# Down projections with more Strassen pairs, whose weight sums are made during the up projections and kept in HBM

## The chip, the cores and the metric

The kernel runs on one core of one Trainium2 chip. The metric is the device time of one execution in microseconds (us). The core has a matrix engine (TensorE, PE in the profile; PEld is its weight load), a vector engine (VectorE, DVE), a scalar engine (ScalarE, ACT), GpSimd (POOL, unused here) and SyncE (SP), whose queue issues the transfers between HBM and the on-chip memory (SBUF). Matmul results accumulate in PSUM.

## The reference

A two-layer encoder on 256 tokens of width 2048 in float32. Each layer is a token mixer followed by a channel mixer, both between RMS norms. Only the channel mixer is touched:

```python
def conv_glu(h, w_up, conv_w, conv_b, w_down):
    u = h @ w_up                                   # 2048 -> 2 * 5632
    gate, val = u[..., :D_FF], u[..., D_FF:]
    gate = depthwise_conv3(gate, conv_w, conv_b)
    return (jax.nn.gelu(gate, approximate=False) * val) @ w_down   # 5632 -> 2048

for i in range(DEPTH):
    ...
    x = x + rms_norm(m, p['mix_post'])
    h = rms_norm(x, p['ffn_pre'])
    x = x + rms_norm(conv_glu(h, *p['ffn']), p['ffn_post'])
```

## The kernel before

Every product is made to nearly full float32 precision from reduced-precision matmuls (type fp32r): each operand is split into a high part and the rest, `hi` and `lo`, and three products are added: hi·hi, hi·lo and lo·hi. The activations are split once. The weights are split as they come in, and this feeds TensorE through the whole program:

- All weights are cut into chunks of 128 rows by 1024 columns (512 KB); `all_chunks` lists them in the order of their use. A chunk holds two blocks of 128x512.
- `_load` lets SyncE fetch a chunk into one of four `raw` buffers (line 162). `_split` casts it on ScalarE into one of five `whi` buffers (line 187) and lets VectorE subtract that from `raw` into one of five `wlo` buffers (line 182). After the subtraction the `raw` buffer is free for the next load; after the chunk's last matmul the `whi` and `wlo` buffers are.
- `weights` is called once a chunk. It issues the splits of up to three chunks and the loads of three more, and hands out the current one. SyncE takes its waits and loads in the order of issue; the order in which an engine gets its other work is set when the program is built.
- `tick`, called after each chunk, runs one step of every generator that was registered with `now`. In this way the vector work of one stage is laid beside the matmuls of another.

The feed-forward block `ffn` runs 11 column groups of 512 (`NFG`). For each, `proj_t` makes the gate half and the value half, with eight chunks each and 16 matmuls a chunk (lines 263 and 265); then VectorE and ScalarE make convolution, GELU and product, and split the result into `gh` and `gl`, the operands of the down projection.

`down` multiplies by the 5632x2048 weights. The 44 row blocks form 22 pairs; the 2048 columns form two halves (`h`) of two column groups (`o`); the tokens form two tiles of 128 (`t`). For one pair and one half this is a 2x2 by 2x2 block product. Plain, it takes eight block products, that is 24 matmuls (lines 1264, 1265 and 1267), from two chunks. By Strassen's rule in Winograd's form it takes seven, 21 matmuls, and needs four sums of weight blocks and four sums of token blocks:

- The class `Seven` loads the two chunks of a pair into buffers of their own (`seven_a`, `seven_b` or `yf`, line 67). Step 0 uses a chunk as it is; then VectorE makes the four weight sums in place (line 81), and steps 1 to 3 use them. So there are 3.5 chunks to split, from two loads.
- `sums` makes the token sums on VectorE, for two pairs at a time, into the tiles `seven`.
- `down_order` writes the order of the chunks out by hand: `LEAD` plain chunks, then for each pair its steps 0 to 3 with plain chunks (`None`) between, then the plain chunks that are left. `PAIRS` says how many of the 22 pairs go by Strassen's rule, by layer and half. The last five chunks of a layer (`HELD`) run one token tile after the other.
- `added` combines the four PSUM banks that Strassen's rule adds, and `done` finishes a half; both are VectorE and ScalarE work that is registered at the last Strassen chunk of the half.

Of the kernel before, what the change touches and what calls it, by code (L numbers as in the profile page):

```python
# [17 lines left out]
P = 128  # L18
# [18 lines left out]

PAIRS = (6, 6), (6, 7)
LEAD = 5, 1


def down_order(h, pairs):

    plain = [("plain", p, o) for o in range(2) for p in range(pairs, KF // 2)]
    out, plain = plain[:LEAD[h]], deque(plain[LEAD[h]:])
    for p in range(pairs):
        for j in (0, None, 1, None, 2, None, 3) if h else (0, None, None, 1, None, 2, 3, None):
            out.append(plain.popleft() if j is None else ("seven", p, j))
    return out + list(plain)


class Seven:

    def __init__(self, a, b):
        self.srcs, self.raw = (a, b), None

    def load(self, model):
        if self.raw is None:
            self.raw = []
            for src, tag in zip(self.srcs, "ab"):
                home = "yf" if tag == "b" and next(model.turns) % 2 else f"seven_{tag}"
                raw = model.room.tile([P, 1024], F32, tag=home, name=f"seven_{tag}", bufs=1)
                model.nc.sync.dma_start(out=raw, in_=src)
                self.raw.append(raw)

    def step(self, model, j):  # L70

        a, b = self.raw
        return (a, a, b, self.t2)[j] if j else a

    def sums(self, model):
        nc = model.nc
        a, b = self.raw
        self.t2 = model.room.tile([P, 512], F32, tag="seven_t", name="seven_t", bufs=1)
        a0, a1, b0, b1 = a[:, :512], a[:, 512:], b[:, :512], b[:, 512:]
        for out, x, y in ((a0, b0, a0), (self.t2, b1, a0), (a1, a1, self.t2), (b0, b1, b0)):  # L80
            nc.vector.tensor_tensor(out=out, in0=x, in1=y, op=ALU.subtract)  # L81


# [8 lines left out]
class Model:  # L92
# [6 lines left out]
    def __init__(self, ctx, tc, a, out):  # L99
        self.tc, self.nc, self.a, self.out = tc, tc.nc, a, out  # L100
        self.soon, self.bg, self.running = [], deque(), []
        self.held = deque()
        self.gate, self.lead, self.led = (), None, 8
        pool = lambda name, **k: ctx.enter_context(tc.tile_pool(name=name, **k))
        self.const = pool("const", bufs=1)
        self.act = pool("act", bufs=1)
        self.wp = pool("wp", bufs=1)
        self.small = pool("small", bufs=2)
        self.ps = pool("ps", bufs=4, space=bass.MemoryType.PSUM)


# [42 lines left out]
    def _load(self, i):  # L154
        if i >= len(self.chunks) or i in self.loaded or i < self.at or i in self.made:
            return
        if isinstance(self.chunks[i], tuple):
            self.chunks[i][0].load(self)
            self.loaded[i] = None
            return  # L160
        raw = self.wp.tile([P, 1024], F32, tag="raw", name="raw", bufs=4)
        self.nc.sync.dma_start(out=raw, in_=self.chunks[i])
        self.loaded[i] = raw

    def _split(self, i, parts=1, late=False):
# [3 lines left out]
        raw = self.loaded.pop(i)  # L169
        seven, step = self.chunks[i] if raw is None else (None, 0)  # L170
        if seven:
            raw = seven.step(self, step)
        if i in self.spot:
# [5 lines left out]

        def low(s=slice(0, 1024)):  # L180
            nc = self.nc
            return nc.vector.tensor_tensor(out=lo[:, s], in0=raw[:, s], in1=hi[:, s].bitcast(F32), op=ALU.subtract)  # L182

        with self.behind(self.gate):
            for j in range(parts):
                s = slice(n * j, n * j + n)
                self.nc.scalar.copy(hi[:, s], raw[:, s])  # L187
                if not late:
                    low(s)
        if seven and step == 0:  # L190
            seven.sums(self)
        self.made[i] = (hi, lo)
# [203 lines left out]
    def spread(self, sp):  # L396

        nc = self.nc
        pb = self.psum("acc")
        for t in range(2):  # L400
            nc.tensor.matmul(pb[:, t * P:(t + 1) * P], self.r[:, t:t + 1].broadcast_to([P, P]), self.ident,
                             start=True, stop=True)
        self.rb = sp.tile([P, T], F32, tag="rb", name="rb", bufs=1)
        nc.vector.tensor_copy(self.rb, pb[:, :T])
# [708 lines left out]
    def ffn(self, layer, pre):  # L1113
        nc, tc = self.nc, self.tc
        with tc.tile_pool(name=f"ffn{layer}", bufs=1) as sp:
            self.room = sp
            xs = self.xhl
            x = lambda k: xs[k // 4][:, k % 4].rearrange("p a t -> p (a t)")
            gh = [sp.tile([P, 4, T], F32R, tag=f"gh{i}", name=f"gh{i}") for i in range(NFG)]
            gl = [sp.tile([P, 4, T], F32R, name=f"gl{i}") for i in range(NFG)]  # L1120
            cw = lambda j, c: self.gain(f"l{layer}_conv_w", j * KF + c)
            gw = sp.tile([P, 4, T], F32, tag="gw", name="gw", bufs=1)
            self.turns = count()
            norm = self.now(self.pre_norm(sp))
            for gi in range(NFG):
                pg = self.proj_t(KD, x, "acc", ROWS[layer] if gi == 0 else 0, gi == 0)
                self.finish(norm)
# [18 lines left out]
                if gi:  # L1146
                    gates()
                pv = self.proj_t(KD, x, "at", after=None if gi else gates)
                for i in range(4):
                    u = self.joined(gw[:, 2 + i % 2], sp.tile([P, T], F32, tag="u", name="u", bufs=2), pv[i])  # L1150
# [3 lines left out]
            self.down(gh, gl, 2 * layer + 1, pre)  # L1154

    def down(self, gh, gl, post, pre):
# [7 lines left out]

        def sums():

            most = max(many)
            for i in range((most + 1) // 2):
                q = min(2, most - 2 * i)
                if q == 1:  # L1170
                    for _ in range(16):
                        yield
                tmp = self.act.tile([P, 2, 512 * q], F32, tag="xm3", name="sums")
                add(tmp[:, 0], gh[i][:, :2 * q].rearrange("p k t -> p (k t)").bitcast(F32),
                    gl[i][:, :2 * q].rearrange("p k t -> p (k t)").bitcast(F32))
                a = tmp[:, 0].rearrange("p (q k t f) -> p q k t f", q=q, k=2, t=2)
# [6 lines left out]
                yield  # L1183
                home, tag = (self.act, f"xm{i}") if i < 3 else (self.room, "gw")
                seven.append(home.tile([P, q, 4, 2, P], F32R, tag=tag, name=f"seven{i}"))
                self.parted(seven[i][:, :, :, 0, :], seven[i][:, :, :, 1, :], s)
                yield
# [4 lines left out]
        def summed(p, n):  # L1192
            return tuple(seven[p // 2][:, p % 2, n, i, :] for i in range(2))

        def operands(kind, p, j, t):

            if kind == "plain":
                return [(2 * j + t, lambda k=2 * p + i: tokens(k, t), i) for i in range(2)]
            if t:
                return []  # L1200
            return [[(4, lambda: tokens(2 * p, 0), 0), (0, lambda: tokens(2 * p + 1, 0), 1)],
                    [(5, lambda: summed(p, 0), 0), (1, lambda: tokens(2 * p + 1, 1), 1)],
                    [(7, lambda: summed(p, 2), 0), (2, lambda: summed(p, 3), 1)],
                    [(6, lambda: summed(p, 1), 0)]][j]

# [31 lines left out]
        gains.append(self.gain_row(post, 0))  # L1237
        self.now(sums())
        ended = None
        for h in range(2):  # L1240
# [29 lines left out]
            for i in range(n):  # L1270
                if i == units[0]:
                    banks += [self.psum("at") for _ in range(4)]
                w = self.weights()
                while items[i][0] == "seven" and len(seven) <= items[i][1] // 2:
                    self.tick()
# [8 lines left out]
            if h == 0:  # L1284
# [49 lines left out]
    def all_chunks(self):  # L1334
# [4 lines left out]

        def down(w, many):  # L1340
            items = []
            for h in range(2):
                pairs = [Seven(w[2 * h, p], w[2 * h + 1, p]) for p in range(many[h])]
                items += [w[2 * h + j, p] if kind == "plain" else (pairs[p], j)
                          for kind, p, j in down_order(h, many[h])]
            return items

        ffn = lambda l: groups(a[f"w_up{l}"], [g for j in range(NFG) for g in (j, NFG + j)]) + \
            down(a[f"w_down{l}"], PAIRS[l])
        out += ffn(0)  # L1350
# [11 lines left out]
def _tiled(w, n=512):  # L1362
# [3 lines left out]
    w = w.reshape(k // (b * P), b, P, m // n, n).transpose(3, 0, 2, 1, 4)  # L1366
    return np.ascontiguousarray(w).reshape(m // n, k // (b * P), P, 1024)


# [57 lines left out]
```

## Time and profile before

| | |
|---|---|
| median of 3 runs | 2049.87 us (2049.73 to 2050.01) |
| the profiled execution | 2049.89 us; span of its instructions 2048.1 us |
| mean granted TensorE clock | 0.998 |
| up projections of layer 0 and 1 | about 344 to 820 us and 1333 to 1810 us |
| down projections of layer 0 and 1 | about 820 to 1058 us and 1810 to 2040 us |
| HBM read, written | 381.96 MB, 2.10 MB |

Times in the profile are in microseconds unless marked ns. "L182" is line 182 of the kernel. In a list of groups a row gives line, engine, operation, the tile written and those read, shapes and count, then the total busy time and the mean duration in ns, and after the bar the engine's idle time just before these instructions and what ended it. In a list of waits a row gives who waited for whom, then us in total, number and longest. A timeline row gives start and length in us, and "x2" means two merged instructions.

### The profile page before, as it was taken

How to read it: one execution, taken by the hardware profiler on the slowest of the kernel's cores; microseconds unless marked ns; L12 is line 12 of the kernel's file. 1: busy time of each engine (PE TensorE's matmuls, PEld its weight loads, DVE VectorE, ACT ScalarE, POOL GpSimd, SP SyncE). 2: the span in 40 equal slices, each digit the busy share in tenths (PEclk: the TensorE clock that was granted, in tenths of full speed). 3: DMA queues.
4: the chain of work that ended last, by engine and by line, in shares of the span. 5: the costliest groups of instructions: out<-in, count | busy, mean ns of one | idle time of the engine just before them, and what ended most of it. 6: DMA issues, size and time to landing. Idle time of an engine off the chain costs nothing.

```text
span 2048.1 us, 29263 instructions
## 1 busy us (share of the span) xinstructions
PE 2035.5 (99%) x10927; PEld 1749.3 (85%) x10927; DVE 1487.1 (73%) x2296; ACT 1133.9 (55%) x1780; POOL 0.2 (0%) x4
## 2 busy tenths in 40 slices
PE   9999999999999999999999999999999999999998
PEld 7888888888888888888888998888888888888886
DVE  6877757766766767978777875676766766797886
ACT  7654546555555555555555664565555555555553
POOL 0000000000000000000000000000000000000000
PEclk9999999999999999999999999999999999999999
DMA  9555566666666666566556445566666666656663
GB/s 335 180 150 161 165 198 201 189 194 193 185 194 189 185 194 191 189 207 211 190 162 188 136 130 171 176 223 190 185 194 193 186 193 190 193 176 216 197 215 122
DMA packets 108718, 385.97 MB, mean 188 GB/s; under 512 B 12064, under 2 KB 12576, under 8 KB 108576
## 3 DMA queue, kind: packets, MB, share of 16 engines
q1 hardware_dynamic: 108288, 383.83, 60.1%
q8 instruction: 85, 1.39, 0.3%
q14 instruction: 57, 0.47, 0.1%
q10 hardware_dynamic: 288, 0.28, 0.0%
HBM read 381.96 MB, written 2.10 MB: 188 GB/s over the span
## 4 chain that ended last, share of the span: by engine, by line
PE 99%; DVE 0%; ACT 0%; DMA 0%; issue 0%; DVEq 0%; SPq 0%
PE ps L263 31%; PE ps L265 15%; PE ps L248 8%; PE ps L246 8%; PE ps L247 8%; PE ps L1265 8%; PE ps L1267 8%; PE ps L1264 8%; PE ps L674 1%; PE ps L332 1%; PE ps L577 1%; PE ps L504 0%; PE ps L584 0%; DMA raw<-in_w_in 0%; PE ps L1004 0%; ACT xhl L727 0%
## 5 line engine op out<-in xcount | busy, mean ns | idle before, releaser
L182 DVE TENSOR_TENSOR wlo<-raw,whi 128x1024 fp32r<-128x1024 f32 (+1 forms) x650 | 792.1, 1221 | 449.8 <-ACT whi L187 444.8
L187 ACT CAST whi<-raw 128x1024 fp32r<-128x1024 f32 (+1 forms) x650 | 681.4, 1050 | 595.8 <-PE ps L263 323.8
L263 PE MATMUL ps<-xhl,whi 128*128 128x512 f32 x2752 | 952.6, 394 | 0.0
L265 PE MATMUL ps<-xhl,wlo 128*128 128x256 f32 x2752 | 757.5, 277 | 0.0
L263 PEld LDWEIGHTS ps<-xhl,whi 128*128 128x128 f32 x2752 | 513.9, 188 | 116.9
L265 PEld LDWEIGHTS ps<-xhl,wlo 128*128 128x128 f32 x2752 | 516.7, 188 | 2.6
L1264 PE MATMUL ps<-whi,gh 128*128 128x512 f32 x579 | 225.5, 389 | 0.0
L1265 PE MATMUL ps<-whi,gl 128*128 128x512 f32 x579 | 225.3, 389 | 0.0
L1267 PE MATMUL ps<-wlo,gh 128*128 128x512 f32 x579 | 180.2, 389 | 0.0
L246 PE MATMUL ps<-whi,xhl 128*128 128x512 f32 x336 | 132.3, 395 | 1.6 <-ACT whi L187 1.6
L247 PE MATMUL ps<-wlo,xhl 128*128 128x512 f32 x336 | 131.4, 391 | 0.0
L248 PE MATMUL ps<-whi,xhl 128*128 128x512 f32 x336 | 130.9, 391 | 0.1
L1264 PEld LDWEIGHTS ps<-whi,gh 128*128 128x128 f32 x579 | 108.7, 188 | 22.6
L1267 PEld LDWEIGHTS ps<-wlo,gh 128*128 128x128 f32 x579 | 108.7, 188 | 22.6
L1265 PEld LDWEIGHTS ps<-whi,gl 128*128 128x128 f32 x579 | 108.7, 188 | 22.4
L246 PE MATMUL ps<-whi,oh 128*128 128x512 f32 x256 | 100.3, 392 | 0.0
L247 PE MATMUL ps<-wlo,oh 128*128 128x512 f32 x256 | 99.7, 390 | 0.0
L248 PE MATMUL ps<-whi,ol 128*128 128x512 f32 x256 | 99.7, 389 | 0.0
L336 ACT COPY gw<-ps 128x256 f32<-128x256 f32 x176 | 64.8, 370 | 42.8 <-PE ps L263 33.8
L187 ACT CAST whi<-seven_a 128x1024 fp32r<-128x1024 f32 x50 | 52.7, 1053 | 62.6 <-DVE seven_a L81 35.3
L182 DVE TENSOR_TENSOR wlo<-seven_a,whi 128x1024 fp32r<-128x1024 f32 x50 | 61.1, 1223 | 20.7 <-ACT whi L187 19.1
L246 PEld LDWEIGHTS ps<-whi,xhl 128*128 128x128 f32 x336 | 63.1, 188 | 14.2 <-ACT whi L187 1.8
(230 smaller groups left out, 2195.4 us busy)
## 6 DMA issues: line engine op xcount, KB each, us to landing
raw<-in_w_up SPq DMA_DIRECT2D x352, 512.0 KB, 4.2
raw<-in_w_down SPq DMA_DIRECT2D x126, 512.0 KB, 4.3
raw<-in_w_in SPq DMA_DIRECT2D x88, 512.0 KB, 4.4
raw<-in_w_out SPq DMA_DIRECT2D x64, 512.0 KB, 3.7
seven_a<-in_w_down SPq DMA_DIRECT2D x25, 512.0 KB, 4.8
seven_b<-in_w_down SPq DMA_DIRECT2D x25, 512.0 KB, 5.2
gb<-in_post SPq DMA_DIRECT2D x16, 256.0 KB, 3.9
raw<-in_w_qn SPq DMA_DIRECT2D x8, 512.0 KB, 3.6
```

Of the source, the lines that this page charges most:

```text
L182: return nc.vector.tensor_tensor(out=lo[:, s], in0=raw[:, s], in1=hi[:, s].bitcast(F32), op=ALU.subtract)
L187: self.nc.scalar.copy(hi[:, s], raw[:, s])
L246: mm(ps, lh, rh, start=start, stop=False)
L247: mm(ps, lh, rl, start=False, stop=False)
L248: return mm(ps, ll, rh, start=False, stop=stop)
L263: ins = mm(out[i], hi[:, s[kk]], x(k), start=k == 0, stop=False, skip_group_check=opening)
L265: ins = mm(out[i][:, :T], lo[:, s[kk]], x(k)[:, :T], start=False, stop=k == nk - 1, skip_group_check=opening)
L332: self.tc.keep_in_program_order(self.nc.tensor.transpose(out, x, self.ident))
L336: self.nc.scalar.copy(b, ps[:, T:])
L1264: mm(bank, xh, w[0][:, c], start=start, stop=False, skip_group_check=loose)
L1265: mm(bank, xl, w[0][:, c], start=False, stop=False, skip_group_check=loose)
L1267: ins = mm(bank, xh, w[1][:, c], start=False, stop=stop, skip_group_check=loose)
```

## The change

The weight sums are made earlier. In `ffn`, from the second column group on, the generator `block_sums` runs beside the up projections, one step a chunk. For every Strassen pair of the layer's down projection it loads the pair's two chunks (1 MB) into one of two buffers (`st` and `g_last`), makes the four sums in place in three VectorE subtractions, and stores both halves in HBM (`blocks`); a job takes seven steps, and two jobs overlap. Host-side, `_paired` lays the four blocks of a pair in one row. In `down` a Strassen pair then has four chunks like any other, all loaded into `raw`: step 0 the two blocks as they are, steps 1 and 2 the stored sums, step 3 one block alone (half a chunk). The class `Seven` goes.

`PAIRS` goes from (6, 6), (6, 7) to (9, 11), (9, 11). In the second half, from the fourth pair on, one plain chunk stands among a pair's steps; elsewhere two do. The token sums for nine pairs are made at the start of `down`, those of two more at the turn of the halves, in `raw` buffers. To find room, `rb` and `u` share the tile `misc`, and the last `gh` and `gl` share the buffer `g_last`.

```diff
-PAIRS = (6, 6), (6, 7)
+PAIRS = (9, 11), (9, 11)
...
-        for j in (0, None, 1, None, 2, None, 3) if h else (0, None, None, 1, None, 2, 3, None):
+        for j in (0, None, 1, 2, 3) if h and p > 2 else (0, None, 1, 2, None, 3):
...
-class Seven:
...
+        self.dram = pool("dram", bufs=1, space=bass.MemoryType.DRAM)
+        self.blocks = {}
...
     def _load(self, i):
-        if isinstance(self.chunks[i], tuple):
-            self.chunks[i][0].load(self)
-            self.loaded[i] = None
-            return
-        raw = self.wp.tile([P, 1024], F32, tag="raw", name="raw", bufs=4)
-        self.nc.sync.dma_start(out=raw, in_=self.chunks[i])
+        src = self.chunks[i]() if callable(self.chunks[i]) else self.chunks[i]
+        raw = self.wp.tile([P, 1024], F32, tag="raw", name="raw", bufs=4)[:, :src.shape[-1]]
+        self.nc.sync.dma_start(out=raw, in_=src)
...
     def _split(self, i, parts=1, late=False):
-        if seven and step == 0:
-            seven.sums(self)
...
     def ffn(self, layer, pre):
+            misc = sp.tile([P, 4, T], F32, tag="misc", name="misc", bufs=1)
+            self.rb = misc[:, 0]
             for gi in range(NFG):
+                if gi == 1:
+                    blocks = self.now(self.block_sums(layer, sp))
...
+                if gi == NFG - 1:
+                    self.finish(blocks)
+                    both = sp.tile([P, 2, 4, T], F32R, tag="g_last", name="g_last", bufs=1)
...
+    def block_sums(self, layer, sp):
+        nc, w = self.nc, self.a[f"w_down{layer}"]
+        jobs = [(h, p) for h in range(2) for p in range(PAIRS[layer][h])]
+        def minus(x, a, b, n=512):
+            nc.vector.tensor_tensor(out=x[:, a:a + n], in0=x[:, b:b + n] if n > 512 else x[:, a:a + n],
+                                    in1=x[:, a:a + n] if n > 512 else x[:, b:b + n], op=ALU.subtract)
+        def half(x, i):
+            return x[:, 1024 * i:1024 * i + 1024]
+        old = None
+        for n in range(len(jobs) + 1):
+            job, new = (jobs[n] if n < len(jobs) else None), None
+            for q in range(7):
+                if job and q == 0:
+                    new = sp.tile([P, 2048], F32, tag=("st", "g_last")[n % 2], name="blocks", bufs=1)
+                if job and q < 2:
+                    nc.sync.dma_start(out=half(new, q), in_=half(w[job[0], job[1]], q))
+                if old and q == 0:
+                    minus(old[1], 1536, 512)
+                    minus(old[1], 0, 1536)
+                    kept = self.blocks[layer, *old[0]] = self.dram.tile([P, 2048], F32, name=...)
+                if old and q in (2, 3):
+                    nc.sync.dma_start(out=half(kept, q - 2), in_=half(old[1], q - 2))
+                    if q == 3 and not job:
+                        return
+                if job and q == 6:
+                    minus(new, 512, 1024, 1024)
+                yield
+            old = (job, new)
...
     def down(self, gh, gl, post, pre):
-        self.now(sums())
+        self.now(sums(many[0]))
...
+                self.now(sums(many[1], True))
...
     def all_chunks(self):
+                    if kind == "plain":
+                        yield w[h, p][:, 1024 * j:1024 * j + 1024]
+                    elif j in (1, 2):
+                        yield lambda h=h, p=p, j=j: self.blocks[layer, h, p][:, 1024 * j - 1024:1024 * j]
+                    else:
+                        yield w[h, p][:, 1536:] if j else w[h, p][:, :1024]
```

More of the change, by code (lines that the diff above doesn't have):

```diff
@@ L2 @@
 from contextlib import ExitStack
-from itertools import count
 import numpy as np
@@ L46, in down_order @@
     for p in range(pairs):
-        for j in (0, None, 1, None, 2, None, 3) if h else (0, None, None, 1, None, 2, 3, None):
+        for j in (0, None, 1, 2, 3) if h and p > 2 else (0, None, 1, 2, None, 3):
             out.append(plain.popleft() if j is None else ("seven", p, j))
     return out + list(plain)
-class Seven:
[L58 to L81, printed above, removed]
 G_NAMES = ["l0_mix_pre", "l0_ffn_pre", "l1_mix_pre", "l1_ffn_pre",
@@ L169, in _split @@
         raw = self.loaded.pop(i)
-        seven, step = self.chunks[i] if raw is None else (None, 0)
-        if seven:
-            raw = seven.step(self, step)
         if i in self.spot:
@@ L178, in _split, with low @@
         n = raw.shape[-1] // parts
-        def low(s=slice(0, 1024)):
+        def low(s=slice(0, raw.shape[-1])):
             nc = self.nc
@@ L402, in spread @@
                              start=True, stop=True)
-        self.rb = sp.tile([P, T], F32, tag="rb", name="rb", bufs=1)
         nc.vector.tensor_copy(self.rb, pb[:, :T])
@@ L1118, in ffn @@
             x = lambda k: xs[k // 4][:, k % 4].rearrange("p a t -> p (a t)")
-            gh = [sp.tile([P, 4, T], F32R, tag=f"gh{i}", name=f"gh{i}") for i in range(NFG)]
-            gl = [sp.tile([P, 4, T], F32R, name=f"gl{i}") for i in range(NFG)]
+            gh = [sp.tile([P, 4, T], F32R, tag=f"gh{i}", name=f"gh{i}") for i in range(NFG - 1)]
+            gl = [sp.tile([P, 4, T], F32R, name=f"gl{i}") for i in range(NFG - 1)]
             cw = lambda j, c: self.gain(f"l{layer}_conv_w", j * KF + c)
             gw = sp.tile([P, 4, T], F32, tag="gw", name="gw", bufs=1)
-            self.turns = count()
+            misc = sp.tile([P, 4, T], F32, tag="misc", name="misc", bufs=1)
+            self.rb = misc[:, 0]
             norm = self.now(self.pre_norm(sp))
+            blocks = None
             for gi in range(NFG):
+                if gi == 1:
+                    blocks = self.now(self.block_sums(layer, sp))
                 pg = self.proj_t(KD, x, "acc", ROWS[layer] if gi == 0 else 0, gi == 0)
@@ L1148, in ffn @@
                 pv = self.proj_t(KD, x, "at", after=None if gi else gates)
+                if gi == NFG - 1:
+                    self.finish(blocks)
+                    both = sp.tile([P, 2, 4, T], F32R, tag="g_last", name="g_last", bufs=1)
+                    gh.append(both[:, 0])
+                    gl.append(both[:, 1])
                 for i in range(4):
-                    u = self.joined(gw[:, 2 + i % 2], sp.tile([P, T], F32, tag="u", name="u", bufs=2), pv[i])
+                    u = self.joined(gw[:, 2 + i % 2], misc[:, 2 + i % 2], pv[i])
                     nc.vector.tensor_tensor(out=u, in0=u, in1=self.rb, op=ALU.mult)
@@ L1154, in ffn @@
             self.down(gh, gl, 2 * layer + 1, pre)
+    def block_sums(self, layer, sp):
[17 more added lines that the diff above has]
+                    minus(old[1], 0, 1536)
+                    kept = self.blocks[layer, *old[0]] = self.dram.tile([P, 2048], F32, name=f"b{layer}{old[0][0]}_{old[0][1]}")
+                if old and q in (2, 3):
[6 more added lines that the diff above has]
+            old = (job, new)
     def down(self, gh, gl, post, pre):
@@ L1163, in down, with sums @@
         many = PAIRS[0 if pre else 1]
[L1165 to L1175, printed above, removed]
+        homes = [(self.act, "xm0", 2), (self.act, "xm1", 2), (self.act, "xm2", 2), (self.room, "st", 2),
+                 (self.room, "gw", 1), (self.room, "yf", 1), (self.room, "misc", 1)]
+        def sums(upto, small=False):
+            while len(seven) < upto:
+                p = len(seven)
+                pool, tag, q = homes.pop(0)
+                k = slice(2 * (p % 2), 2 * (p % 2) + 2 * q)
+                if small:
+                    tmp = self.wp.tile([P, 2, 512], F32, tag="raw", name="sums", bufs=4)
+                else:
+                    tmp = self.act.tile([P, 2, 512 * q], F32, tag="xm3", name="sums")
+                add(tmp[:, 0], gh[p // 2][:, k].rearrange("p k t -> p (k t)").bitcast(F32),
+                    gl[p // 2][:, k].rearrange("p k t -> p (k t)").bitcast(F32))
                 a = tmp[:, 0].rearrange("p (q k t f) -> p q k t f", q=q, k=2, t=2)
@@ L1183, in sums @@
                 yield
-                home, tag = (self.act, f"xm{i}") if i < 3 else (self.room, "gw")
-                seven.append(home.tile([P, q, 4, 2, P], F32R, tag=tag, name=f"seven{i}"))
-                self.parted(seven[i][:, :, :, 0, :], seven[i][:, :, :, 1, :], s)
+                home = pool.tile([P, q, 4, 2, P], F32R, tag=tag, name=f"seven{p}")
+                self.parted(home[:, :, :, 0, :], home[:, :, :, 1, :], s)
+                seven.extend(home[:, i] for i in range(q))
                 yield
@@ L1192, in summed @@
         def summed(p, n):
-            return tuple(seven[p // 2][:, p % 2, n, i, :] for i in range(2))
+            return tuple(seven[p][:, n, i, :] for i in range(2))
         def operands(kind, p, j, t):
             if kind == "plain":
-                return [(2 * j + t, lambda k=2 * p + i: tokens(k, t), i) for i in range(2)]
+                return [(2 * j + t, lambda k=2 * p + i: tokens(k, t), i if j else 1 - i) for i in range(2)]
             if t:
                 return []
[L1201 to L1204, printed above, removed]
+            return [[(0, lambda: tokens(2 * p + 1, 0), 0), (4, lambda: tokens(2 * p, 0), 1)],
+                    [(1, lambda: tokens(2 * p + 1, 1), 0), (5, lambda: summed(p, 0), 1)],
+                    [(7, lambda: summed(p, 2), 0), (6, lambda: summed(p, 1), 1)],
+                    [(2, lambda: summed(p, 3), 0)]][j]
         def added(h, at):
@@ L1273, in down @@
                 w = self.weights()
-                while items[i][0] == "seven" and len(seven) <= items[i][1] // 2:
+                while items[i][0] == "seven" and len(seven) <= items[i][1]:
                     self.tick()
@@ L1338, in all_chunks, with down @@
         out += [a["w_out0"][g, c] for g in range(4) for c in (4, 5, 6, 7, 0, 1, 2, 3)]
-        def down(w, many):
-            items = []
+        def down(layer, w, many):
             for h in range(2):
[L1343 to L1346, printed above, removed]
+                for kind, p, j in down_order(h, many[h]):
+                    if kind == "plain":
+                        yield w[h, p][:, 1024 * j:1024 * j + 1024]
+                    elif j in (1, 2):
+                        yield lambda h=h, p=p, j=j: self.blocks[layer, h, p][:, 1024 * j - 1024:1024 * j]
+                    else:
+                        yield w[h, p][:, 1536:] if j else w[h, p][:, :1024]
         ffn = lambda l: groups(a[f"w_up{l}"], [g for j in range(NFG) for g in (j, NFG + j)]) + \
-            down(a[f"w_down{l}"], PAIRS[l])
+            list(down(l, a[f"w_down{l}"], PAIRS[l]))
         out += ffn(0)
@@ L1367, in _tiled, with _paired @@
     return np.ascontiguousarray(w).reshape(m // n, k // (b * P), P, 1024)
+def _paired(w):
+    w = _tiled(w)
+    w = w.reshape(2, 2, *w.shape[1:3], 2, 512)
+    return np.concatenate([w[:, o, :, :, k] for o, k in ((0, 1), (0, 0), (1, 0), (1, 1))], axis=-1)
 def _rope(pos, dim):
@@ L1406 @@
         arr[f"w_up{l}"] = _tiled(inp[f"l{l}_w_up"])
-        arr[f"w_down{l}"] = _tiled(inp[f"l{l}_w_down"])
+        arr[f"w_down{l}"] = _paired(inp[f"l{l}_w_down"])
     arr["w_in1"] = _tiled(inp["l1_w_in"][:, :1024])
```

## The prediction

> **What bounds the kernel now.** I read the page from its head down: the shares of the engines, then the chain that ended last.
>
> ```profile
> span 2048.1 us, 29263 instructions
> PE 2035.5 (99%) x10927; PEld 1749.3 (85%) x10927; DVE 1487.1 (73%) x2296; ACT 1133.9 (55%) x1780; POOL 0.2 (0%) x4
> PE 99%; DVE 0%; ACT 0%; DMA 0%; issue 0%; DVEq 0%; SPq 0%
> ```
>
> The chain is TensorE (PE) from end to end. A busy PE is partly modelled, so the waits of PE were next. These are all it has, 4.1 us together, and none is in a down projection:
>
> ```profile
> PE ps L246 <- ACT whi L187: 1.6, 1, 1.6
> PE ps L332 <- issue: 1.1, 1, 1.1
> PE ps L230 <- DVE zeros L1326: 1.1, 1, 1.1
> PE ps L504 <- DVE x L496: 0.3, 1, 0.3
> ```
>
> So a product removed from PE is a gain for as long as the weights arrive in time. How near they are to late is in the windows: opening, up projections, down projections of layer 0 and of layer 1 (length; busy us of PE, PEld, DVE, ACT, POOL; clock; DMA share; GB/s).
>
> ```profile
> 10.00:15.00 5.00, 5.00 (x22) 3.83 (x22) 5.00 (x9) 4.82 (x8) 0.00 (x0) 1.00 1.04 413
> 25.00:30.00 5.00, 5.00 (x23) 4.14 (x23) 3.09 (x3) 4.61 (x9) 0.00 (x0) 1.00 1.01 339
> 377.00:800.00 423.00, 423.00 (x2443) 369.93 (x2442) 288.91 (x458) 227.76 (x343) 0.00 (x0) 1.00 0.64 190
> 820.00:1058.00 238.00, 238.00 (x1058) 197.07 (x1057) 189.81 (x233) 125.77 (x152) 0.00 (x0) 1.00 0.59 196
> 1810.00:2035.00 225.00, 225.00 (x994) 186.31 (x993) 183.86 (x219) 119.19 (x137) 0.00 (x0) 1.00 0.57 187
> ```
>
> An up chunk has 16 matmuls: 423 us / (2443/16) = 2.77 us. VectorE (DVE) is at 68% there and 80% in down; DMA moves under 200 GB/s where 339 to 413 have been seen.
>
> **The change, part by part.** *Products (gain).* The pace of one plain chunk in down, from PE's timeline, twelve matmuls between the two rows:
>
> ```profile
> 999.61 0.39 PE L1264 MATMUL ps<-whi,gh 128*128 128x512 f32 x1
> ...
> 1002.33 0.39 PE L1264 MATMUL ps<-whi,seven 128*128 128x512 f32 x1
> ```
>
> (1002.33 − 999.61)/12 = 0.227 us a matmul, though each lasts 0.39. A pair of weight blocks takes 24 matmuls plain and 21 by Strassen's rule. The pairs go from 6+6+6+7 = 25 to 9+11+9+11 = 40, so 45 matmuls go: 45 × 0.227 = **10.2 us**. The Trainium skill ("TensorE: Matmul & The Clock Gate", the section "Wait — 56ns, not 53.3ns?") gives 215.7 ns for 512 columns at the warm clock; by it the estimate is 9.7 us. The row decides, and the clock in the windows is 1.00.
>
> *Weights in down (loss).* Before, a Strassen pair loaded two chunks into tiles of its own and VectorE made the sums in place. Afterwards it loads 3.5 chunks (the sums come back from HBM), all through the four `raw` buffers. A `raw` buffer is reloaded only when the VectorE `wlo` of its chunk is done; SyncE's waits show that this is what every load waits for, and the page has the parts of the round trip (bytes of a load and median to landing; mean ns of cast and subtraction, 1024 and 512 wide):
>
> ```profile
> SPq L162 <- DVE wlo L182: 1187.5, 501, 9.0
> raw<-in_w_down SPq DMA_DIRECT2D x126, 512.0 KB, 4.3
> seven_a<-in_w_down SPq DMA_DIRECT2D x25, 512.0 KB, 4.8
> seven_b<-in_w_down SPq DMA_DIRECT2D x25, 512.0 KB, 5.2
> gb<-in_post SPq DMA_DIRECT2D x16, 256.0 KB, 3.9
> L182 DVE TENSOR_TENSOR wlo<-raw,whi 128x1024 fp32r<-128x1024 f32 (+1 forms) x650 | 792.1, 1221 | 449.8 <-ACT whi L187 444.8
> L187 ACT CAST whi<-raw 128x1024 fp32r<-128x1024 f32 (+1 forms) x650 | 681.4, 1050 | 595.8 <-PE ps L263 323.8
> L182 DVE TENSOR_TENSOR wlo<-seven_t,whi 128x512 fp32r<-128x512 f32 x25 | 17.2, 689 | 13.8 <-ACT whi L187 13.8
> L187 ACT CAST whi<-seven_t 128x512 fp32r<-128x512 f32 x25 | 15.6, 623 | 29.9 <-PE ps L1265 28.2 <-DVE wlo L182 1.6
> ```
>
> How long a landing takes depends on what is in flight. The view of `raw` gives least, median and most in us, first from 889 to 895 us, where loads come singly, then from 895 to 900, inside a burst whose issues stand below it:
>
> ```profile
> DMA to landing us min/median/max: 3.6/3.7/3.9
> ...
> DMA to landing us min/median/max: 4.6/5.0/5.4
> ...
> 895.79 0.33 SPq L162 DMA_DIRECT2D raw<-in_w_down  x1
> 896.92 0.33 SPq L67 DMA_DIRECT2D seven_a<-in_w_down  x1
> 898.38 0.33 SPq L162 DMA_DIRECT2D raw<-in_w_down  x1
> 899.74 0.33 SPq L67 DMA_DIRECT2D seven_b<-in_w_down  x1
> ```
>
> The demand: in the second half from the fourth pair on, a unit is the chunks 0, plain, 1, 2, 3 with 21 + 12 = 33 matmuls, 33 × 0.227 = 7.48 us for five chunks. With four buffers each round may last 4 × 7.48/5 = 5.98 us. The supply: landing + cast 1.05 + subtraction 1.22. With about three of four buffers in flight at spacings near 1.7 us I take 4.8 us, the median of `seven_a`, which comes behind two others: 7.07 us for a whole chunk; for the half one 3.9 + 0.62 + 0.69 = 5.21. Mean (4 × 7.07 + 5.21)/5 = 6.70, a unit takes 5/4 × 6.70 = 8.37 us, 0.89 longer than PE needs. Eight such units a layer, two layers: 16 × 0.89 = **14.3 us**. The other units (0, plain, 1, 2, plain, 3) need 45 × 0.227 = 10.2 us; the ring gives (5 × 7.07 + 5.21)/6 × 6/4 = 10.1: even, 0 us. Bounds: at 3.7 us the mean is 5.82, under 5.98, and the loss is 0; at 5.4 the tails lose 23.9 us and the 24 other units 0.69 each, 16.6. The break-even landing is 3.9 us.
>
> *VectorE at the start of down (loss).* The sums on token blocks grow from 3 groups (4 in layer 1) to 5 before the first half, then two more small ones. Already now the first chunk after the first Strassen step is nearly late: its subtraction ends at 835.70, its first use on PE is at 835.94.
>
> ```profile
> 834.48 1.22 DVE L182 TENSOR_TENSOR wlo<-raw,whi 128x1024 fp32r<-128x1024 f32 x1
> ...
> 835.94 0.62 PE L1267 MATMUL ps<-wlo,gh 128*128 128x512 f32 x2
> ...
> L1159 DVE TENSOR_TENSOR sums<-gh,gl 128x1024 f32<-128x1024 f32 (+1 forms) x7 | 8.0, 1144 | 1.2 <-PE ps L265 1.2
> L1159 DVE TENSOR_TENSOR sums<-sums 128x256 f32<-128x256 f32 (+1 forms) x28 | 10.0, 400 | 0.1
> L723 DVE TENSOR_TENSOR seven<-sums,seven 128x1024 fp32r<-128x1024 f32 (+1 forms) x7 | 8.0, 1143 | 0.0
> L81 DVE TENSOR_TENSOR seven_t<-seven_b,seven_a 128x512 f32<-128x512 f32 x25 | 17.3, 691 | 0.6
> ```
>
> A group is 1.14 + 4 × 0.40 + 1.14 = 3.9 us. One and a half more groups (5.8 us) fall into the first Strassen unit; the four weight sums of a pair (4 × 0.69 = 2.8 us) leave it, and so do two plain chunks, with 2.4 us of VectorE but 5.4 us of PE. Net that is 5.8 − 2.8 − 2.4 + 5.4 = 6.0 us of lateness, against a lead of four chunks' splits (the estimate under the second rival is 3.7 us). Between 0 and 6.0 a layer, nearer to the 2.3 that is left over; I take 1.5, since the groups need not stand ahead of the splits, so **3 us**.
>
> *Turn of the halves (loss).* The evacuation of the first half already keeps VectorE from any weight for 7.4 us:
>
> ```profile
> 928.44 1.22 DVE L182 TENSOR_TENSOR wlo<-seven_a,whi 128x1024 fp32r<-128x1024 f32 x1
> ...
> 937.10 1.22 DVE L182 TENSOR_TENSOR wlo<-raw,whi 128x1024 fp32r<-128x1024 f32 x1
> ```
>
> Weight sums of 2.8 us leave this stretch; two small groups (about half of 3.9 each) come in and take two turns of the `raw` ring. Between 0 and 3.9 a layer; I take 1.5, **3 us**. After that no lead is left for the tail units, so I credit none.
>
> *Sums in the up projections (hidden).* Each of 40 jobs has two loads, two stores and three subtractions (one 1024 wide, two 512: 1.22 + 2 × 0.69 = 2.6 us) over seven chunks, 19.4 us. VectorE goes from 68% to 82%. DMA gets 2.1 MB more per 19.4 us, 190 + 108 = 298 GB/s. What hides it: a `raw` buffer has 4 × 2.77 = 11.1 us for a round that takes 4.2 + 2.3 = 6.5 us. The jobs' issues go through SyncE's one queue, ahead of the weight loads behind them; a store waits for subtractions emitted two chunks earlier, and the next weight load waits for a later VectorE instruction anyway. Were the cover gone, four loads and four stores in four chunks (4.2 MB in 11.1 us) would at the 339 GB/s above take 12.4 us, 1.3 us a job: 51 us over all.
>
> *Small edits at nothing.* `rb` and `u` move into one tile, the last `gh` and `gl` into one whose previous user stored 16 chunks earlier; the chunks' column order only renames blocks. They cost a wait only if a store took over 40 us.
>
> **The sum.** The profiled execution took 2049.89 us (span 2048.1 and 1.8 around it), 0.02 above the median. 2049.9 − 10.2 + 14.3 + 3 + 3 = **2060 us**.
>
> **The rivals.** *The ring keeps up (faster).* If landings stay under 3.9 us at the higher rate, the tails lose nothing and most of the 10.2 us arrives: 2049.9 − 10.2 + 0 to 3, about 2041. For it: single loads land in 3.7, and DMA can carry 413 GB/s where the tail asks 4.5 × 0.524 MB/7.48 us = 315. Against it: every burst in down, the only place with such spacing, is at 4.6 or more. The Trainium skill ("DMA: Bandwidth & Descriptors", section "Anatomy of one DMA") fits a transfer as about 2.0 us + bytes/436 GB/s, by estimate 3.2 us for 512 KB whatever is in flight, and would settle for this rival; the trace has 3.6 as the least here and 5.0 in the burst, so I follow the trace.
>
> *The lead pays (same).* Five pairs of `whi`/`wlo` let the splits run four chunks ahead, 4 × 1.5 = 6 us less the 2.3 of a split: 3.7 us a tail. If VectorE is not as late at the start and the turn as I say (3 us in all), −10.2 + 14.3 − 7.4 + 3 = −0.3: 2049.6. For it: no PE wait in down now, although VectorE is as crowded. Against: the units before the tail run even, so a lead once lost does not return.
>
> *The up projections become bound by supply (far slower).* The 51 us above in place of cover: 2060 + 51 = 2111, or 2085 if half of it is absorbed. It decides where a landing goes over 11.1 − 2.3 = 8.8 us; the median there is now 4.2:
>
> ```profile
> raw<-in_w_up SPq DMA_DIRECT2D x352, 512.0 KB, 4.2
> ```
>
> **How the numbers follow.** Ring late: 0.52, own range 2054 to 2078. Ring keeps up: 0.26. Lead pays: 0.15. Up bound by supply: 0.07. The range must reach to the first rival and leaves out the last: 2040 to 2078. A difference of 0.2% (4.1 us) is about what a measurement of this kernel can tell from none. Faster is the first rival and the lower edge of the second, 0.28; same 0.14; slower 0.58.
>
> **What would show it.** Right: PE waits in down for `whi` or `wlo`, most of them after the fourth pair of each second half, some 7 us in each tail; ScalarE's casts there end their waits on the DMA of `raw`, no longer on PE; `raw` from the stored sums lands in 4.6 to 5.0 us; matmuls 45 fewer in the lines of down at the same 0.227; no PE wait in the up projections, DMA near 300 GB/s there. Wrong: landings below 4 us at spacings of 1.5 us, or ScalarE in the tails still waiting for PE; then the gain stands. PE waits between 390 and 800 us would speak for the last rival.

## The result and the profile after

The changed kernel takes 2119.65 us (median of 4 runs, 2115.0 to 2124.62) against 2049.92 us: ratio 1.0341, 95% interval 1.0311 to 1.0371. It is 70 us slower, where 10 were forecast. The profiled execution is the shortest of the four, 2115.0 us. Its page has, of the rows shown before:

```profile
span 2113.2 us, 29789 instructions
PE 2061.7 (98%) x10882; PEld 1734.5 (82%) x10882; DVE 1561.4 (74%) x2388; ACT 1159.2 (55%) x1817; POOL 0.2 (0%) x4
PE 79%; DMA 12%; DVE 5%; ACT 3%; issue 1%; ACTq 0%; DVEq 0%; SPq 0%
```

TensorE is no longer the whole chain: 12% of it is DMA, 8% VectorE and ScalarE. What PE and its weight loads wait for is now the split weights of down (lines 1269 and 1272 are the products there):

```profile
PE ps L1269 <- ACT whi L149: 25.0, 34, 1.7
PE ps L1272 <- DVE wlo L144: 6.9, 2, 3.8
...
PEld ps L1269 <- ACT whi L149: 44.8, 52, 2.1
PEld ps L1272 <- DVE wlo L144: 37.5, 67, 4.3
```

What the casts in down wait for is mostly the landing of the load, no longer a buffer that PE holds (L1270 is a product of down):

```profile
ACT whi L149 <- DMA raw<-in_w_down: 129.1, 106, 3.5
ACT whi L149 <- DMA raw<-b: 71.0, 66, 3.2
ACT whi L149 <- PE ps L1270: 14.8, 12, 3.0
```

The longest pieces of the chain in order of time (start, length) show the ring itself: a subtraction frees a `raw` buffer, the next load goes into it at once, lands, is cast (1.06 us, between the rows) and subtracted.

```profile
1004.37 1.24 DVE wlo L144
1005.62 5.33 DMA raw<-b
1012.13 1.24 DVE wlo L144
1013.38 4.88 DMA raw<-in_w_down
1019.44 1.24 DVE wlo L144
1020.70 4.18 DMA raw<-in_w_down
```

From load to load into the same buffer are 7.76 and 7.32 us, and only four loads fit into that. The landings on the page (`b` are the stored sums):

```profile
raw<-in_w_up SPq DMA_DIRECT2D x352, 512.0 KB, 5.0
raw<-in_w_down SPq DMA_DIRECT2D x136, 512.0 KB, 4.7
...
raw<-b SPq DMA_DIRECT2D x80, 512.0 KB, 6.4
...
raw<-in_w_down SPq DMA_DIRECT2D x40, 256.0 KB, 4.5
```

Where the time went can be counted. From the starts of PE's matmuls in the lines of down (996 a layer, 1020 and 1017 before), each stretch of the hand-written order has a length; less 0.2267 us a matmul, this is lost:

| stretch | matmuls a layer | lost, layer 0 | lost, layer 1 | forecast, both |
|---|---|---|---|---|
| 5 plain chunks, first 3 units | 195 | 0.0 | 0.0 | 3 |
| 6 further units of the first half | 270 | 4.8 | 6.7 | 0 |
| turn: 4 plain chunks | 48 | 1.7 | 2.4 | 3 |
| first 3 units of the second half | 135 | 5.4 | 3.6 | 0 |
| 8 dense units (0, plain, 1, 2, 3) | 264 | 17.1 | 20.5 | 14.3 |
| 2 plain and 5 held chunks | 84 | 7.2 | 6.7 | 0 |
| sum | 996 | 36.2 | 39.9 | 20.3 |

Together 76.1 us are lost. Less the 10.2 us of the products that went, that is 65.9 us; the span grew by 65.1. The up projections take 487.57 us in each layer, from first to last matmul, as before.

### The profile page after: what moved, and what is told of

It is laid out like the page before. It is cut to its first block, busy times and chain, and to the rows that moved or that the text cites. A ratio compares the mean times of both kernels' runs of the same rounds, so it can differ in the third digit from the quotient of the medians.

```text
span 2113.2 us, 29789 instructions
## 1 busy us (share of the span) xinstructions
PE 2061.7 (98%) x10882; PEld 1734.5 (82%) x10882; DVE 1561.4 (74%) x2388; ACT 1159.2 (55%) x1817; POOL 0.2 (0%) x4
## 4 chain that ended last, share of the span: by engine, by line
PE 79%; DMA 12%; DVE 5%; ACT 3%; issue 1%; ACTq 0%; DVEq 0%; SPq 0%
PE ps L223 30%; PE ps L225 15%; PE ps L208 8%; PE ps L206 8%; PE ps L207 8%; DMA raw<-in_w_down 7%; DMA raw<-b 5%; DVE wlo L144 4%; ACT whi L149 2%; PE ps L1272 2%; PE ps L1269 2%; PE ps L1270 2%; PE ps L633 1%; PE ps L292 1%; DVE m L1160 1%
## 5 line engine op out<-in xcount | busy, mean ns | idle before, releaser
L144 DVE TENSOR_TENSOR wlo<-raw,whi 128x1024 fp32r<-128x1024 f32 (+1 forms) x780 | 924.8, 1193 | 415.9 <-ACT whi L149 402.6
L149 ACT CAST whi<-raw 128x1024 fp32r<-128x1024 f32 (+1 forms) x780 | 796.2, 1027 | 690.1 <-PE ps L223 156.2
L1269 PE MATMUL ps<-whi,gh 128*128 128x512 f32 x440 | 177.2, 403 | 24.7 <-ACT whi L149 21.7
L1270 PE MATMUL ps<-whi,gl 128*128 128x512 f32 x440 | 172.7, 392 | 0.0
L1272 PE MATMUL ps<-wlo,gh 128*128 128x512 f32 x440 | 146.5, 407 | 9.9 <-DVE wlo L144 6.9
L1130 DVE TENSOR_TENSOR blocks<-blocks 128x512 f32<-128x512 f32 (+1 forms) x120 | 103.6, 865 | 69.2 <-DMA blocks<-in_w_down 49.2
L1269 PEld LDWEIGHTS ps<-whi,gh 128*128 128x128 f32 x440 | 83.0, 189 | 59.1 <-ACT whi L149 39.0
L1272 PEld LDWEIGHTS ps<-wlo,gh 128*128 128x128 f32 x440 | 79.6, 189 | 47.1 <-DVE wlo L144 33.5
L296 ACT COPY gw<-ps 128x256 f32<-128x256 f32 x176 | 62.3, 369 | 67.8 <-DVE gw L297 23.9
L1270 PEld LDWEIGHTS ps<-whi,gl 128*128 128x128 f32 x440 | 83.1, 189 | 16.1
L206 PEld LDWEIGHTS ps<-whi,xhl 128*128 128x128 f32 x336 | 63.1, 188 | 14.0 <-ACT whi L149 1.8
L208 PEld LDWEIGHTS ps<-whi,xhl 128*128 128x128 f32 x336 | 62.9, 188 | 13.8 <-DVE xhl L687 0.7
```

What stands on the lines that cost most here:

```text
L206: mm(ps, lh, rh, start=start, stop=False)
L208: return mm(ps, ll, rh, start=False, stop=stop)
L296: self.nc.scalar.copy(b, ps[:, T:])
L1130: nc.vector.tensor_tensor(out=x[:, a:a + n], in0=x[:, b:b + n] if n > 512 else x[:, a:a + n], in1=x[:, a:a + n] if n > 512 else x[:, b:b + ...
L1269: mm(bank, xh, w[0][:, c], start=start, stop=False, skip_group_check=loose)
L1270: mm(bank, xl, w[0][:, c], start=False, stop=False, skip_group_check=loose)
```

## The experiments

All ratios are to the kernel before, run on the same chips.

| run | median us (least to most) | ratio, 95% interval |
|---|---|---|
| e1_from_w | 2113.39 (2104.5 to 2126.38) | 1.0295 (1.0265 to 1.0326) |
| e2_six_pairs | 2050.59 (2050.3 to 2058.8) | 1.0007 (0.9998 to 1.0017) |
| e3_nine_raw4 | 2083.32 (2079.53 to 2091.13) | 1.0168 (1.0146 to 1.019) |
| e4_nine_raw6 | 2043.61 (2043.35 to 2052.3) | 0.9979 (0.9969 to 0.9988) |
| e5_eleven_raw6 | 2042.26 (2040.97 to 2052.73) | 0.9973 (0.9963 to 0.9984) |
| e6_nine_raw5 | 2043.79 (2043.13 to 2044.86) | 0.9972 (0.9961 to 0.9982) |
| e7_no_sums | 2107.56 (2105.52 to 2108.75) | 1.0281 (1.0268 to 1.0294) |
| e8_eleven_spaced | 2050.5 (2041.79 to 2062.78) | 1.0005 (0.999 to 1.0021) |
| e9_eleven_no_sums | 2041.86 (2040.86 to 2042.5) | 0.9961 (0.9949 to 0.9972) |
| e10_eleven_shift | 2042.39 (2040.82 to 2048.73) | 0.9971 (0.9959 to 0.9983) |

**Is it the place of the stored sums in HBM?**

```diff
-  yield lambda h=h, p=p, j=j: self.blocks[layer, h, p][:, 1024 * j - 1024:1024 * j]
+  yield w[h, p][:, 1024 * j - 1024:1024 * j]
```

> Steps 1 and 2 of a Strassen pair read the raw weights of the pair instead of the stored sums (same shape, size, stride and order); the sums are still made and stored, so only what those two loads read is changed, and the output lacks the sums. Theory 1 (the stored sums' own place in HBM makes their landing late): the loads of steps 1 and 2 land like the other weight loads in down, at 4.4 to 5.0 us instead of 6.4; the mean round of a raw buffer falls from 7.5 to about 6.9 us and the waits of TensorE in down fall from 75 us to 25 to 40: 2065 to 2080 us. Theory 2 (the landing is late because the four loads bunch in the ring, whatever they read): landing stays at 6 us or more, time 2110 to 2125. Theory 3 (the vector work is late, not the loads): 2110 to 2125 and the casts in down wait for something else than the DMA.

2113 us: theory 2. Sorted by their place in the order, the loads of steps 1 and 2 land after 5.9 and 6.4 us (medians of 40) although they read ordinary weights; from the stored sums they took 6.2 and 6.8. Steps 0 and 3 are at 4.4 and 4.5 in this run, plain chunks at 4.8. Two such loads, step 1 and step 2 of one pair, as the view of `raw` has them (least, median, most):

```profile
DMA to landing us min/median/max: 6.5/6.8/7.2
```

The casts in down wait for the DMA in this run too, so theory 3 is out. The landing is late by the place in the ring: the subtraction of step 3, half a chunk, runs right behind that of step 2 and takes 0.7 us, so the buffers for steps 1 and 2 of the next pair come free 0.6 us apart. In the dense units (0, plain, 1, 2, 3) three or four loads are in flight for 69% of the time and a single one for 7 to 9%.

The execution that was profiled here is the longest of its four (2126.38 us). Down loses 38 and 36 us in it, as in the changed kernel, but the up projections take 497.0 and 491.5 us, 13.4 more than in the other profile.

**Does storing the sums cost by itself?** Edit: `PAIRS` (6, 6), (6, 6) and the order of before.

> The changed kernel with 6 Strassen pairs in every half and the order of the kernel before (seven or eight chunks a unit with three or four plain ones). Theory 1 (the round through four raw buffers is the bound, only where a unit gives it under about 7.5 us): 8 chunks in 69 x 0.227 = 15.6 us allow 7.8 us a round, so next to no wait of TensorE in down: 2050 to 2058 us (one pair less than before costs 0.7). Rival (making, storing and reloading the sums costs by itself, in the up projections or by DMA load): 2075 us or more.

2050.59 us, the time of before within its interval; nine of the ten executions lie within 0.6 us and one is at 2058.8. 24 pairs by way of HBM cost no more than 25 made in place. The windows show what that includes: 244 GB/s instead of 193 in up, and no PE idle. The first row is up in layer 0 of the kernel before, then come up and down of layer 0 in this run.

```profile
345.00:820.00 475.00, 475.00 (x2744) 415.44 (x2743) 329.71 (x525) 262.19 (x398) 0.00 (x0) 1.00 0.64 193
...
345.00:820.00 475.00, 475.00 (x2744) 415.27 (x2743) 355.74 (x561) 261.41 (x398) 0.00 (x0) 1.00 0.74 244
820.00:1058.00 238.00, 238.00 (x1058) 197.16 (x1057) 162.04 (x186) 127.46 (x152) 0.00 (x0) 1.00 0.74 240
```

**Four, five and six buffers at nine pairs.** Three runs with `PAIRS` (9, 9), (9, 9) and the units 0, plain, 1, 2, plain, 3 throughout. With nine pairs the tiles `yf` and `misc` are free in down; two of the runs load into them as well:

```diff
+  if k >= 8 and k % 6 > 3:       # k: place of the chunk in down; five buffers: k % 5
+      raw = self.room.tile([P, 1024], F32, tag=("yf", "misc")[k % 6 - 4], ...)
+  else:
       raw = self.wp.tile([P, 1024], F32, tag="raw", name="raw", bufs=4)
```

> Nine pairs in every half, two plain chunks in each unit: 36 pairs, so 33 matmuls fewer than before, 7.5 us. Theory 1 (ring of four): every unit allows 4 x 10.2/6 = 6.8 us a round where 7.4 are needed, 0.9 us lost a unit, 36 units: 2042 + 32, 2065 to 2085 us. Rival (only the dense units of the second half are late): 2045 to 2055.

> Nine pairs in every half, five load buffers (only yf added). Theory (round trip over the number of buffers): a round may last 5 x 10.2/6 = 8.5 us, and 7.5 to 7.9 are needed, so most of the 40 us that four buffers lose goes: 2043 to 2053 us. Rival (a threshold of another kind, such as the bunching that six buffers happen to break): 2060 us or more.

> As the run with nine pairs, but from the ninth chunk of each down projection on two of six loads go to two more buffers (the tiles yf and misc, free there with nine pairs), so six loads are under way instead of four. Theory 1 (the round trip, that is latency over the number of buffers): a round may last 10.2 us a unit, TensorE's waits in down fall under 8 us: 2041 to 2050 us. Rival (DMA or HBM carries no more: more loads in flight only land later): within 8 us of the run with four buffers.

Four: 2083 us. Five: 2043.8. Six: 2043.6. This is the round trip over the number of buffers. With four, 6.8 us a round are allowed and the ring is slower; with five 8.5, and it isn't. In the run with six no unit loses anything, the casts wait for PE again, and the loads land evenly (5.2 and 5.3 us), later for plain chunks and step 0 and earlier for the stored sums than in the changed kernel (4.7 and 6.4). In the mean they land no earlier: over the six units of the first half that lose time with four buffers, a load lands after 5.3 us with four and 5.5 with five or six. What the buffers change is how long it may take. The waits, then the DMA issues, of the run with six:

```profile
ACT whi L153 <- PE ps L1274: 144.1, 139, 2.1
```

```profile
raw<-in_w_down SPq DMA_DIRECT2D x140, 512.0 KB, 5.2
...
raw<-b SPq DMA_DIRECT2D x72, 512.0 KB, 5.3
```

**Six buffers at nine and eleven pairs: the better version.** The order and the pairs of the change. The token sums of pairs 9 and 10 go to `xm0` once the second half has done with pairs 0 and 1, so `yf` and `misc` are left for loads:

```diff
-  (self.room, "gw", 1), (self.room, "yf", 1), (self.room, "misc", 1)]
+  (self.room, "gw", 1)]
...
+  late.append(self.act.tile([P, 2, 4, 2, P], F32R, tag="xm0", name="late"))   # for small
...
-  self.now(sums(many[1], True))   # at the turn of the halves
...
+  if h and items[i] == ("seven", 1, 3):
+      self.now(sums(many[1], True))
```

> The changed kernel with its 9 and 11 pairs and its order, and six load buffers in down: from the ninth chunk on two of six loads go to yf and misc, and the token sums of pairs 9 and 10 of the second half go to xm0 once its first four... two pairs there are through (a little later than before). Theory (the round trip over four buffers is the whole loss): the dense units allow 6 x 7.48/5 = 9.0 us a round where about 7.7 are needed (landing 5.3, as with nine pairs and six buffers); TensorE's waits in down fall from 76 to under 10 us: 2040 to 2050 us, faster than the kernel before if the end of each layer isn't late. Rival (in the dense units DMA itself is the bound, 315 GB/s asked): landings over 6.5 us and 15 us or more still lost in the tails, 2055 us or more.

2042.26 us, the least 2041.0. The median is 77 us under the changed kernel and 7.5 under the kernel before, with an unchanged number of products, loads and sums. All 20 units of a layer lose 0.0 us; 2.2 are left at the end of layer 0. The two kernels in the same stretch of dense units, the changed kernel first (209 matmuls in 47 us are PE's full pace):

```profile
979.00:1026.00 47.00, 42.03 (x163) 28.47 (x162) 26.77 (x25) 23.56 (x25) 0.00 (x0) 1.00 0.77 244
```

```profile
979.00:1026.00 47.00, 47.00 (x209) 38.91 (x208) 35.98 (x33) 31.41 (x34) 0.00 (x0) 1.00 0.93 321
```

DMA carries 321 GB/s where it carried 244, so neither DMA nor HBM was the limit. This run differs from the changed kernel in two things, the buffers and the later sums; the three runs with nine pairs differ in the buffers alone. Its executions spread from 2040.97 to 2052.73 us, and two of the twelve are no shorter than the kernel before.

**What do the sums cost in up?** The run of the first experiment without the sums (`block_sums` is not started):

> As the run that read raw weights in steps 1 and 2, and the sums are not made either: no loads, subtractions or stores for them in the up projections. The output lacks the sums. Theory (the up projections hide the sums; the loss is in down): up projections 487.6 us each as before, 70 to 80 us of waits in down, 2105 to 2120 us. Rival (the work in the up projections costs, at the end of up or by late lead): under 2095 us.

2107.56 us, in the expected range. Down still loses 32.9 us in layer 0 and 33.4 in layer 1, so nearly all of the loss stands without a single sum made. The up projections' own loads land at 4.2 us instead of 5.0. The executions spread over 3 us only, where those of the changed kernel spread over 10. The same with six buffers:

> As the run with eleven pairs and six buffers, but no sums are made and steps 1 and 2 read the raw weights (output lacks the sums). If the up projections hide the sums: 2041 us as its fastest executions, the spread gone if the jobs cause it. Rival (down at 315 GB/s causes the spread): the spread of 10 us stays. If the sums cost something in every execution: under 2040 us.

2041.86 us with a spread of 1.6 us. The least times with and without the sums are the same (2040.97 and 2040.86), but with them the times go up to 2052.73. Where that spread comes from, two runs tried to find. One spread a job's transfers out:

```diff
-  if job and q < 2:               # loads
+  if job and q in (1, 4):
...
-  if old and q in (2, 3):         # stores
+  if old and q in (3, 6):
...                                # all three subtractions in steps 0 and 1 of the next job
```

> As the run with eleven pairs and six buffers, but a job's two loads and two stores in the up projections stand two or three chunks apart instead of next to each other, and its three subtractions in the first two steps of the next job. If the spread of that run (2041 to 2053 us) comes from bursts of the jobs' transfers that at times make the up projections late: median 2041 us and a spread under 3 us. Rival (the spread comes from the down projections, or from the added DMA load however it is spread): median and spread as before, 2041 to 2053.

It got slower, 2050.5 us, with a spread of 21: the remedy was wrong. Its profiled execution (2053.26 us) has a stretch in which the loss can be seen (in the last section): the up projections of layer 0 take 498.1 us there, while down loses 3.3 us in all. The other left loads and stores in place and made the subtractions one step later:

```diff
+  if old and q == 0:
+      minus(old[1], 512, 1024, 1024)
-  if old and q == 0:
+  if old and q == 1:
       minus(old[1], 1536, 512)
       minus(old[1], 0, 1536)
...
-  if job and q == 6:
-      minus(new, 512, 1024, 1024)
```

> As the run with eleven pairs and six buffers, but the 1024 wide subtraction of a job comes one step later (first step of the next job's turn) and the two 512 wide ones one step later too; loads and stores stay where they were. In that run VectorE stood 28 us for the landing of the jobs' loads and 52 us of SyncE went to the landing of the stores, both in the up projections. If VectorE's wait with the weight subtractions behind it causes the slow executions: VectorE's waits for the jobs' loads fall under 15 us, median 2041 to 2042 us, spread under 6 us. Rival (SyncE's wait for the stores, with the weight loads behind it, causes them): spread 2041 to 2053 us stays.

2042.39 us, spread 7.9 us: no difference that can be told from the run before it, and VectorE's wait for the jobs' loads didn't fall (27.7 us there, 50.4 here), so this run doesn't separate it from SyncE's wait for the jobs' stores; the waits of both in this run:

```profile
DVE blocks L1134 <- DMA blocks<-in_w_down: 50.4, 13, 6.0
```

```profile
SPq L1147 <- DMA b<-blocks: 53.6, 22, 6.9
```

## Why the prediction was wrong

*Right:* the sign and the main mechanism. 45 matmuls fewer (996 + 996 against 1020 + 1017), at an unchanged pace, worth 10.2 us: with six buffers 7.5 to 9 us of it arrive. The ring of four `raw` buffers is the bound, PE waits in down for `whi` and `wlo`, and the casts wait for the DMA of `raw`. The store in HBM is harmless in up in the profiled execution, with DMA at 280 GB/s between 400 and 800 us. The three longer executions, up to 2124.62 us, were not profiled.

*The step that failed.* The sum had 20.3 us of loss and 76.1 were measured; 23.3 of the difference lie in the dense units. What failed is the landing in the round trip of "Weights in down", 4.8 us for every whole chunk and 3.9 for the half one, 4.62 in the mean. Over the 80 loads of the dense units the mean is 5.51 us. Step 0 and the plain chunk land after 4.5 and 4.2 (medians there), but steps 1 and 2, which go out close together, after 6.4 and 7.0, and the half chunk after 5.7. Cast and subtraction take 2.08 us, as forecast; another 0.36 us pass between the parts of a round, for which the sum had nothing. So a round takes 7.9 us from load to load instead of 6.70, and a unit 9.83 instead of 8.37: 37.6 us lost in place of 14.3. "Three of four buffers in flight" was right: a dense load has 1.9 others beside it in the mean. The landing at that number was too short. The 4.8 was the median of 25 `seven_a` loads; over all loads with two others the kernel before already has 5.2 (table in the last section), by which the prediction's own sum gives 2077 us.

*The same landing cost more elsewhere.* "Even, 0 us" for the units with two plain chunks stood on 6.76 us against 6.80, a margin of 0.04. With a mean landing of 5.3 us, where 4.65 were forecast, these units lose 11.5 us in the first half. And the two plain and five held chunks at the end of a layer, which the prediction didn't cost at all, lose 13.9, nearly all of it in the held chunks: their first token tile takes a chunk every 1.36 us, while VectorE evacuates the half. With six buffers 2.2 us of this are left.

*The two terms of VectorE.* The sums at the start of down (3 us) lost 0.0. The turn of the halves (3 us) was too small, and part of it came later than the table's row of that name. The four plain chunks there lose 4.1 us, but also 3.6 with nine pairs and four buffers, where no small groups of token sums are made; so that is mostly the ring. The three units behind them lose 9.0 us in the changed kernel and 0.9 in that run, with the same order of chunks. What differs there are the two small groups, made in `raw` buffers from 945 to 956 us in layer 0, so they cost some 8 us. No run moves them alone, so this is a comparison and not a test.

*The rivals.* "The lead pays" and "the ring keeps up" are out: five split pairs hid the lateness for three units. The time lies above even the 2111 us of "the up projections become bound by supply", but it isn't that mechanism: up is as long as before in the profiled execution, and without any sums the kernel still takes 2107.56 us. The fit of a transfer as 2.0 us + bytes/436 GB/s (the Trainium skill, "DMA: Bandwidth & Descriptors", "Anatomy of one DMA"), 3.2 us for a load here by estimate, would have had the ring keep up. The section gives it for transfers that GpSimd issues, and these are SyncE's; the runs have 3.6 us for a load alone and medians of 4.2 to 7.0 in the dense units. The range ended at 2078, below the prediction's own bounds: a landing of 5.4 us, with the other terms as forecast, adds up to 2049.9 − 10.2 + 23.9 + 16.6 + 6 = 2086 us.

## What to carry to other kernels

When loads are made smaller or denser in time, divide the round trip of a buffer (landing, then every step until it is free) by the number of buffers, and compare it with the time of one load's work in the densest stretch, not in the mean. Take the landing from all loads that have as many others in flight as the change will have, and allow for its scatter. A margin of a few per cent is none: at 6.76 us against 6.80 the units lost about 1 us each. One more buffer (2083 to 2044 us) did more than the whole saving of arithmetic.

## What the runs showed of the hardware

A wait of TensorE can cost more than its length. In the run with spaced jobs PE stands still for 2.6 us and then runs at about half its pace for 3.4 us: from one 512-column product to the next are 0.64 us (501.66 to 502.30), where at full pace it is 0.36 (504.76 to 505.12). PE's timeline (start, length, instruction):

```profile
498.29 0.39 PE L227 MATMUL ps<-xhl,whi 128*128 128x512 f32 x1
501.28 0.58 PE L229 MATMUL ps<-xhl,wlo 128*128 128x256 f32 x1 [2.60 <-DVE wlo L148]
501.66 0.63 PE L227 MATMUL ps<-xhl,whi 128*128 128x512 f32 x1
502.09 0.41 PE L229 MATMUL ps<-xhl,wlo 128*128 128x256 f32 x1
502.30 0.63 PE L227 MATMUL ps<-xhl,whi 128*128 128x512 f32 x1
...
504.76 0.40 PE L227 MATMUL ps<-xhl,whi 128*128 128x512 f32 x1
505.00 0.28 PE L229 MATMUL ps<-xhl,wlo 128*128 128x256 f32 x1
505.12 0.39 PE L227 MATMUL ps<-xhl,whi 128*128 128x512 f32 x1
```

The windows around it (the granted clock is the third number from the end, ahead of the DMA share and GB/s):

```profile
495.00:500.00 5.00, 3.68 (x21) 2.93 (x20) 4.05 (x9) 2.57 (x6) 0.00 (x0) 1.00 0.81 293
500.00:505.00 5.00, 3.72 (x12) 3.20 (x13) 5.00 (x9) 3.56 (x6) 0.00 (x0) 0.66 0.83 301
505.00:510.00 5.00, 5.00 (x30) 4.36 (x29) 5.00 (x7) 2.11 (x2) 0.00 (x0) 1.00 0.88 251
```

The changed kernel has such a place at the end of layer 0, clock 0.92 and 0.82, in the held chunks that lost 7.2 us:

```profile
1062.00:1070.00 8.00, 4.86 (x17) 3.31 (x17) 8.00 (x11) 5.54 (x8) 0.00 (x0) 0.92 0.61 170
1070.00:1076.00 6.00, 6.00 (x23) 4.83 (x22) 4.98 (x8) 2.75 (x5) 0.00 (x0) 0.82 0.92 327
```

The Trainium skill describes this gate ("TensorE: Matmul & The Clock Gate", "What's actually happening"): half clock after at least one idle window of about 3.4 us, full clock after a busy one of the same length. The trace agrees in the 3.4 us of slow running; here an idle time of 2.6 us was enough, and 3.1 us in the changed kernel.

The second thing is how far a landing depends on a load's neighbours: in the first experiment 512 KB from the same tensor landed in 4.4 us as step 0 and in 6.4 as step 2. Sorted by the number of other transfers in flight (weight loads and the jobs' loads and stores, in the mean over the load's own landing, rounded), the medians of the 512 KB weight loads into `raw` agree from kernel to kernel, in us:

| others in flight | 0 | 1 | 2 | 3 | 4 | 5 |
|---|---|---|---|---|---|---|
| kernel before | 3.6 | 4.3 | 5.2 | 5.7 (2 loads) | | |
| changed kernel | 3.6 | 4.3 | 5.2 | 5.7 | 6.9 | 7.9 |
| eleven pairs, six buffers | 3.6 | 4.3 | 5.1 | 5.8 | 6.6 | 7.5 |

The number doesn't settle a single landing: with two others, eight of ten loads of the changed kernel take between 4.3 and 6.9 us.

What stays open is the cause of the spread of 12 us with the sums made (21 us with the jobs spaced). In the two long executions that were profiled the time lies in the up projections, where the jobs run: 13.4 us more than at full pace with raw weights read, 11.2 with spaced jobs. The five executions without sums spread by 1.6 us only, but so do the seven with nine pairs and five buffers (1.7 us), for which sums are made. Whether VectorE's waits for the jobs' loads or SyncE's for their stores make the spread was not settled.
